# Down-projection of two wide layers in three sweeps of seven block products, with weight sums made by GpSimd during attention

## The chip, the cores and the metric

The kernel runs on one core of one Trainium2 chip. The metric is the time of one execution on the device in microseconds. Five engines work side by side, each through its own list of instructions in order: PE (TensorE, matmuls), DVE (VectorE), ACT (ScalarE), POOL (GpSimd) and SP (SyncE, which here issues most of the DMAs). An instruction that waits for a semaphore holds up everything behind it on its engine.

## The reference

The model is a small encoder over 512 tokens of width 1024: an attention layer with two head groups, a squared-ReLU MLP of width 4096, a neighbourhood attention layer, a second MLP of the same size, and a final norm, all in float32. The part in question is the MLP, which stands in both layers:

```python
def sq_relu_mlp(h, w_up, w_down):
    u = jax.nn.relu(h @ w_up)
    return (u * u) @ w_down          # w_up: 1024 x 4096, w_down: 4096 x 1024

h = x
for layer in range(DEPTH):           # DEPTH = 2
    hn = rmsnorm(h, norm_mix[layer])
    h = h + (hybrid_attention(hn, ...) if layer % 2 == 0 else neighbourhood_attention(hn, ...))
    h = h + sq_relu_mlp(rmsnorm(h, norm_ffn[layer]), ffn_w_up[layer], ffn_w_down[layer])
return rmsnorm(h, final_norm)
```

## The kernel before

Tokens lie along the free dimension: `hT` holds the residual as 8 tiles of 128 features x 512 tokens. Every float32 product is done as three matmuls: each operand is split into a rounded high half and the remainder (ACT copies the high half, DVE subtracts for the low one), and high x high, high x low and low x high are added up in PSUM (`mm3`, lines 501 to 503). So each weight chunk is loaded by SP into a raw tile, split by ACT (L212) and DVE (L202), and used by PE.

**Seven products.** Where two input tiles, two output tiles and both halves of the tokens are taken as 2 x 2 blocks, seven block products of 256 columns replace eight (class `Seven`, matmuls in L388 to L390). Weights and tokens then need sums of blocks first. In the first product of an MLP (1024 to 4096), `seven_chunk` loads two 128 x 256 weight blocks and lets GpSimd make the sums (L302 to L304); the token sums are made once.

**The MLP.** The 4096 hidden features are 32 tiles. The second product (4096 to 1024) takes them in stages: `SIZES` says how many tiles each stage has. In the first wide layer 6, 8 and 8 tiles go through the plain second product with 512-column matmuls, and 10 are kept raw (not split) and go through seven products over 256 output columns at a time, four times. In the second wide layer it is 6, 8, 6 plain, 8 raw, and 4 more tiles that the last part (`last_mlp`, `down`) takes plain, with the tokens on the partitions, so that the final norm follows from them. Beside the last plain stage, `convert` lets DVE and ACT make the sums and splits of the raw tiles.

**Attention in front.** The first attention walks through 64 steps (16 heads x 4 token blocks). A step is: scores on PE, negated maximum and scaling on DVE (L1001), exponential on ACT, reciprocal on DVE, and the scaling of the 512 probabilities of each row by GpSimd (L1005); three steps later PE transposes them (L972), and PE multiplies by the values (L985). A list of other work (`fill`) is dealt out between the steps, a share per step: projections of the second head group, then the first half of the output projection. The second half (`out_proj` with k0 = 4, again lines 501 to 503) needs the last heads and comes behind the attention, and behind it the first wide layer. The second attention has 16 heads of two half steps each (`rest`); there the order of PE, ACT, DVE and GpSimd is the order in which it is written, and GpSimd scales 256 probabilities at a time (L1430) and issues some moves of keys and queries.

**What sets the order.** Outside the second attention a scheduler orders each engine's instructions. On SP it alone does, everywhere. Weight chunks are asked for up to five chunks ahead of their use and split two ahead; a load waits for its buffer (four raw buffers, or one of 30 slots of 128 x 1024). PE's program never skips an instruction that waits.

## Time and profile before

| what | value |
|---|---|
| median of 3 runs | 1183.32 us (1182.38 to 1185.65) |
| span of the profiled execution | 1184.0 us (the page gives no other time for it) |
| PE busy | 1160.5 us, 98% |
| DVE, ACT, GpSimd busy | 883.2, 640.3, 526.1 us |
| DMA | 128.01 MB moved, 108 GB/s in the mean |
| first attention's scalings on GpSimd | 77.6 to 244.3 us |
| first matmul of the first wide layer | 267.89 us |
| second attention's scalings | 641.8 to 808.1 us |
| matmuls of L501 to L503 (512 columns) | about 0.23 us apart |

The stages in time: input projection and first attention to about 268 us, first wide layer to about 604, second attention with its projections to about 831, second wide layer to the end. A row of stretches gives the busy time of each engine in it, with PE's granted clock, the share of time in which DMA was busy, and what it moved. A row of a timeline gives the start in us, how long it took, engine, line, what it writes and reads, and in brackets how long the engine stood idle before it and what released it.

### The profile page before, as it was taken

Reading aid. Unit: us, or ns where it says so; the run is one execution under the profiler, and the core shown is the slowest. Engines: PE = TensorE matmul, PEld = TensorE weight load, DVE = VectorE, ACT = ScalarE, POOL = GpSimd, SP = SyncE. Lnnn points to the kernel's source line nnn. Section 1 sums busy time; section 2 is a strip of 40 time slices with the busy share of each in tenths; the row PEclk is TensorE's granted clock in tenths of the full one; section 3 lists DMA queues with packets and bytes.
Section 4 is the critical chain, followed back from the end, with each engine's and each line's share of the span. In section 5 each row is a group of like instructions: output and inputs, shape, how many; then the busy total and the mean of one; then the engine's idle time right before and its main releaser. Section 6 shows DMA issues by size and latency. Waiting matters only on the chain.

```text
span 1184.0 us, 19784 instructions
## 1 busy us (share of the span) xinstructions
PE 1160.5 (98%) x7128; PEld 1021.2 (86%) x7128; DVE 883.2 (75%) x1514; ACT 640.3 (54%) x1081; POOL 526.1 (44%) x662
## 2 busy tenths in 40 slices
PE   9989999999999999999999999999999999999997
PEld 8667778888899899988998998988889989998895
DVE  5788998878967368786884676667996736778975
ACT  4468676664546247562553565555554624666344
POOL 3267343224562377819602232231376625774710
PEclk9999999999999999999999999999999999999998
DMA  7223225212524723225226464433352341322412
GB/s 244 71 54 92 68 78 134 62 56 77 167 86 134 263 70 90 72 90 165 67 72 178 131 184 126 116 112 109 107 165 76 115 134 55 98 64 89 143 36 71
DMA packets 110145, 128.01 MB, mean 108 GB/s; under 512 B 9075, under 2 KB 86816, under 8 KB 110048
## 3 DMA queue, kind: packets, MB, share of 16 engines
q1 hardware_dynamic: 106992, 119.30, 33.5%
q0 software_dynamic: 2304, 6.31, 2.2%
q8 instruction: 56, 0.92, 0.3%
q10 hardware_dynamic: 752, 1.15, 0.3%
q14 instruction: 41, 0.34, 0.1%
HBM read 104.32 MB, written 6.29 MB: 93 GB/s over the span
## 4 chain that ended last, share of the span: by engine, by line
PE 81%; DVE 4%; ACT 1%; issue 1%; POOL 0%; DVEq 0%; ACTq 0%
PE mm L503 8%; PE mm L501 8%; PE mm L502 8%; PE mm L390 4%; PE mm L389 4%; PE mm L388 4%; PE t L388 3%; PE t L389 3%; PE t L390 3%; PE s L502 2%; PE s L503 2%; PE s L501 2%; PE s L390 2%; PE s L388 2%; PE s L389 2%; PE s L997 2%
## 5 line engine op out<-in xcount | busy, mean ns | idle before, releaser
L309 DVE TENSOR_TENSOR wlo<-a,whi 128x896 fp32r<-128x896 f32 x132 | 161.8, 1230 | 83.7 <-ACT whi L308 82.9
L308 ACT ACTIVATE whi<-a 128x896 fp32r<-128x896 f32 x132 | 125.0, 950 | 155.0 <-PE o L502 45.8
L501 PE MATMUL mm<-a,whi 128*128 128x512 f32 x485 | 195.9, 406 | 0.9 <-DVE a L915 0.7
L503 PE MATMUL mm<-a,wlo 128*128 128x512 f32 x485 | 192.1, 397 | 2.5 <-DVE wlo L202 2.5
L502 PE MATMUL mm<-a,whi 128*128 128x512 f32 x485 | 192.5, 397 | 0.1
L202 DVE TENSOR_TENSOR wlo<-raw,whi 128x1024 fp32r<-128x1024 f32 (+4 forms) x117 | 139.3, 1193 | 66.4 <-ACT whi L212 63.9
L212 ACT ACTIVATE whi<-raw 128x1024 fp32r<-128x1024 f32 (+3 forms) x120 | 116.4, 971 | 92.2 <-PE s L502 39.8
L302 POOL TENSOR_TENSOR a<-a 128x128 f32<-128x128 f32 x132 | 85.1, 645 | 173.3 <-DMA a<-in_ffn_w_up_dram 103.9
L303 POOL TENSOR_TENSOR a<-a 128x256 f32<-128x256 f32 x132 | 120.2, 910 | 10.3
L304 POOL TENSOR_TENSOR a<-a 128x128 f32<-128x128 f32 x132 | 115.1, 872 | 10.3
L503 PEld LDWEIGHTS mm<-a,wlo 128*128 128x128 f32 x485 | 91.7, 189 | 23.7 <-DVE wlo L202 3.4
L501 PEld LDWEIGHTS mm<-a,whi 128*128 128x128 f32 x485 | 91.8, 189 | 20.4 <-PE t L972 0.9
L502 PEld LDWEIGHTS mm<-a,whi 128*128 128x128 f32 x485 | 91.9, 190 | 17.4 <-DVE a L545 0.4
L388 PE MATMUL mm<-a,whi 128*128 128x256 f32 x370 | 103.9, 281 | 0.0
L389 PE MATMUL mm<-a,whi 128*128 128x256 f32 x370 | 103.9, 281 | 0.0
L390 PE MATMUL mm<-a,wlo 128*128 128x256 f32 x370 | 103.7, 280 | 0.0
L1005 POOL TENSOR_SCALAR p<-p,ti 128x512 f32<-128x512 f32 x64 | 46.2, 724 | 92.3 <-DVE ti L1004 81.1
L1430 POOL TENSOR_SCALAR p<-p,ti 128x256 f32<-128x256 f32 x64 | 35.6, 567 | 104.8 <-DVE ti L1429 91.8
L388 PE MATMUL t<-a,whi 128*128 128x256 f32 x264 | 74.2, 281 | 0.0
L389 PE MATMUL t<-a,whi 128*128 128x256 f32 x264 | 74.1, 281 | 0.0
L390 PE MATMUL t<-a,wlo 128*128 128x256 f32 x264 | 73.9, 280 | 0.0
L390 PEld LDWEIGHTS mm<-a,wlo 128*128 128x128 f32 x370 | 69.6, 188 | 0.2 <-DVE wlo L309 0.2
(338 smaller groups left out, 3210.8 us busy)
## 6 DMA issues: line engine op xcount, KB each, us to landing
a<-in_ffn_w_up_dram SPq DMA_DIRECT2D x104, 256.0 KB
raw<-in_ffn_w_down_dram SPq DMA_DIRECT2D x46, 512.0 KB
raw<-in_od_w_qkv_dram SPq DMA_DIRECT2D x64, 128.0 KB
a<-in_ffn_w_down_dram SPq DMA_DIRECT2D x28, 256.0 KB
raw<-in_ffn_w_up_dram SPq DMA_DIRECT2D x12, 512.0 KB
raw<-in_ev_w_in_dram SPq DMA_DIRECT2D x12, 384.0 KB
a<-a SPq DMA_DIRECT2D x18, 256.0 KB
bias<-bx SPq DMA_DIRECT2D x16, 256.0 KB
```

What stands on the lines that cost most here:

```text
L202: z = lambda: (eng or DVE).tensor_tensor(to, src, f32(high), op=ALU.subtract)
L212: ACT.activation(hi[:, 0:m], raw[:, 0:m], AF.Copy)
L303: POOL.tensor_tensor(r[:, 4:6], r[:, 2:3].to_broadcast([P, 2, P]), r[:, 0:7:6], op=ALU.add)
L304: POOL.tensor_tensor(r[:, 7], r[:, 3], r[:, 5], op=ALU.subtract)
L308: ACT.activation(hi[:, 0:896], raw[:, 128:1024], AF.Copy)
L309: DVE.tensor_tensor(lo[:, 0:896], raw[:, 128:1024], f32(hi[:, 0:896]), op=ALU.subtract)
L388: PE.matmul(o, wh, x[:, 0], start=kp == 0 and n in (0, 1, 3, 5), stop=False, skip_group_check=True)
L389: PE.matmul(o, wh, x[:, 1], start=False, stop=False, skip_group_check=True)
L390: PE.matmul(o, wl, x[:, 0], start=False, stop=kp == self.np - 1, skip_group_check=True)
L501: PE.matmul(o, wh, xh, start=first, stop=False)
L502: PE.matmul(o, wh, xl, start=False, stop=False)
L503: PE.matmul(o, wl, xh, start=False, stop=last)
```

## The change

`FIRST, RAW, MORE = 6, (26, 22), (0, 4)` takes the place of `SIZES`: in both wide layers only the first 6 tiles go through the plain second product; all others but the last 4 of the second layer are kept raw, 26 and 22 tiles, that is 13 and 11 pairs. All output columns are now handled at once: the seven products of a pair are over blocks of 512 output columns and 256 tokens, done in three sweeps over all pairs (two, two and three products), whose sums stay in six PSUM banks until a sweep ends.

The sums of the weight blocks are no longer made on the way. `SumsAhead` makes them during the attention in front: per pair of weight tiles SP loads two tiles of 512 KB, GpSimd does four additions or subtractions of 512 elements per partition, and SP writes each result (256 KB) to a buffer in DRAM (`made`), from which the second and the third sweep read; the first reads the original weights, and the third also half a tile of them. In the first attention two such steps are called per attention step from step 36 on; in the second, one after each scaling of GpSimd. The sums of token blocks are made by GpSimd in place within the sweeps, and DVE and ACT split them one pair ahead; `convert` is gone, and the transposes of the residual for the final norm move from the second product into `down`.

```diff
+    FIRST, RAW, MORE = 6, (26, 22), (0, 4)
...
+    class SumsAhead:
...
+        def load(self, kp):
+            if kp < self.n:
+                self.raw[kp] = Slot(F32), Slot(F32)
+                for z, s_ in enumerate(self.raw[kp]):
+                    k = self.k0 + 2 * kp + z
+                    SP.dma_start(s_.t, self.w[k * P : (k + 1) * P, :])
+
+        def steps(self):
+            self.load(0)
+            yield
+            for kp in range(self.n):
+                self.load(kp + 1)
...
+                POOL.tensor_tensor(a22, a21, a22, op=ALU.add)
+                SP.dma_start(line(to[0, :, S:]), a22)
+                yield
+                POOL.tensor_tensor(a21, a11, a21, op=ALU.subtract)
+                SP.dma_start(line(to[1, :, 0:S]), a21)
+                yield
+                POOL.tensor_tensor(a11, a22, a11, op=ALU.subtract)
+                SP.dma_start(line(to[0, :, 0:S]), a11)
+                yield
+                POOL.tensor_tensor(a12, a12, a11, op=ALU.subtract)
+                SP.dma_start(line(to[1, :, S:]), a12)
...
         fill.run(1.5)
+        if n >= 36:
+            next(sums0, None)
+            next(sums0, None)
...
-    SIZES = (6, 8, 8, 10), (6, 8, 6, 8, 4)
...
+    def sweep_chunk(w, k0, kind, made):
...
+        if kind == 0:
+            for z in range(2):
+                SP.dma_start(line(a[:, S * z : S * z + S]), half(k0 + z, 0))
+        else:
+            SP.dma_start(a, made[kind - 1])
+        if kind == 2:
+            SP.dma_start(line(b[:, 0:S]), half(k0 + 1, 1))
+        yield
...
+        ACT.activation(hi, a, AF.Copy)
+        DVE.tensor_tensor(lo, a, f32(hi), op=ALU.subtract)
...
+    class Sweeps:
...
+            if kind == 0:
+                split_to(d[:, :, 0], d[:, :, 1], r[:, 0:4:2])
+                POOL.tensor_tensor(r[:, 0:2], r[:, 1:4:2], r[:, 0:2], op=ALU.subtract)
+                POOL.tensor_tensor(s2, r[:, 3], r[:, 0], op=ALU.subtract)
...
+                wh, wl = hi[:, c : c + P], lo[:, c : c + P]
+                PE.matmul(o, wh, x[:, 0], start=first and m % 2 == 0, stop=False, skip_group_check=True)
+                PE.matmul(o, wh, x[:, 1], start=False, stop=False, skip_group_check=True)
+                PE.matmul(o, wl, x[:, 0], start=False, stop=last, skip_group_check=True)
...
+        reserve[0] = 3
+        sweeps = []
+        R, V = stage(0, RAW[l], MORE[l], lambda: sweeps.append(Sweeps(w, FIRST, made)))[1:]
+        reserve[0] = 6
+        beside = last(FIRST + RAW[l], V) if last else lambda kind, kp: next(bias, None)
+        for kind, kp in sweeps[0].run(R):
+            beside(kind, kp)
...
             for x in w:
                 norm(*x)
+                next(sums1, None)
```

The scheduler moves instructions around the edits. In the rows below a line number is that of the program it comes from; names are tiles, `a` being a slot.

GpSimd at the end of the first attention. Before, the last softmax scalings stand together, and the first sums of the wide layer's weights follow:

```order
L1005 TENSOR_SCALAR p_2709<-p_2709,ti_2708 128x512
L1005 TENSOR_SCALAR p_2742<-p_2742,ti_2741 128x512
L1005 TENSOR_SCALAR p_2759<-p_2759,ti_2758 128x512
L1005 TENSOR_SCALAR p_2787<-p_2787,ti_2786 128x512
L1005 TENSOR_SCALAR p_2804<-p_2804,ti_2803 128x512
L302 TENSOR_TENSOR a_3414<-a_3414 128x128
```

With the change (scaling is L1050, the four sums of a pair are L806, L809, L812 and L815):

```order
L1050 TENSOR_SCALAR p_2889<-p_2889,ti_2888 128x512
L806 TENSOR_TENSOR a_2636<-a_2635,a_2636 128x2x256
L809 TENSOR_TENSOR a_2635<-a_2635 128x2x256
L812 TENSOR_TENSOR a_2635<-a_2636,a_2635 128x2x256
L815 TENSOR_TENSOR a_2636<-a_2636,a_2635 128x2x256
L1050 TENSOR_SCALAR p_2910<-p_2910,ti_2909 128x512
L1050 TENSOR_SCALAR p_2942<-p_2942,ti_2941 128x512
L806 TENSOR_TENSOR a_2708<-a_2707,a_2708 128x2x256
L1050 TENSOR_SCALAR p_2961<-p_2961,ti_2960 128x512
L809 TENSOR_TENSOR a_2707<-a_2707 128x2x256
```

The last of these scalings is the 64th; 41 of the 52 sums stand ahead of it and 11 behind it, the first of them right behind the 35th scaling, 16 ahead of the 43rd, none between the 49th and the 55th, and 28 behind the 55th.

SP around the loads for the second half of the output projection (`raw<-in_ev_w_out_dram 128x2x512`). Before, these loads stand among the moves of keys and queries:

```order
L866 DMA a_2188<-a_2126 32x1024
L863 DMA a_2222<-a_2221 64x1024
L190 DMA raw_2880<-in_ev_w_out_dram 128x2x512
L885 DMA a_2271<-a_2270 64x1024
L866 DMA a_2221<-a_2126 32x1024
L885 DMA a_2303<-a_2302 64x1024
L887 DMA a_2270<-a_620 32x1024
L190 DMA raw_2882<-in_ev_w_out_dram 128x2x512
L887 DMA a_2302<-a_620 32x1024
L190 DMA raw_2948<-in_ev_w_out_dram 128x2x512
L190 DMA raw_2950<-in_ev_w_out_dram 128x2x512
L190 DMA raw_3065<-in_ffn_w_up_dram 128x2x512
```

With the change:

```order
L816 DMA made_621<-a_2781 128x2x256
L807 DMA made_621<-a_2842 128x2x256
L810 DMA made_621<-a_2841 128x2x256
L813 DMA made_621<-a_2841 128x2x256
L816 DMA made_621<-a_2842 128x2x256
L190 DMA raw_3037<-in_ev_w_out_dram 128x2x512
L190 DMA raw_3039<-in_ev_w_out_dram 128x2x512
L190 DMA raw_3105<-in_ev_w_out_dram 128x2x512
L190 DMA raw_3107<-in_ev_w_out_dram 128x2x512
L190 DMA raw_3222<-in_ffn_w_up_dram 128x2x512
```

All four loads now stand behind the last write of the sums; that write waits for the last sum of GpSimd.

PE at the end of the first attention. Before, matmuls of the second half of the output projection (weights `whi_2884`, from `raw_2880`) stand between transposes and value products:

```order
L972 MATMUL t_2830<-cst,p_2759 128x128 x4
L502 MATMUL mm_2878<-a_2185,whi_2884 128x512
L972 MATMUL t_2848<-cst,p_2787 128x128 x4
L503 MATMUL mm_2878<-a_2185,wlo_2885 128x512
L501 MATMUL s_2879<-a_2185,whi_2884 128x512
L502 MATMUL s_2879<-a_2185,whi_2884 128x512
L503 MATMUL s_2879<-a_2185,wlo_2885 128x512
L985 MATMUL o_2837<-a_2809,a_2310 128x256
```

With the change (weights `whi_3041`, from `raw_3037`; value products are L1030):

```order
L1030 MATMUL o_2994<-a_3003,a_2373 128x256
L1030 MATMUL o_2994<-a_3004,a_2373 128x256
L1030 MATMUL o_2994<-a_3003,a_2430 128x256
L1030 MATMUL o_2994<-a_3004,a_2430 128x256
L501 MATMUL mm_3033<-a_2232,whi_3041 128x512
L502 MATMUL mm_3033<-a_2232,whi_3041 128x512
L503 MATMUL mm_3033<-a_2232,wlo_3042 128x512
L501 MATMUL mm_3034<-a_2232,whi_3041 128x512
```

The first matmul with these weights now comes behind the last value product; to the first matmul of the wide layer the work of PE is the same in both, and up to the transposes behind the 44th scaling its order is too.

More of the change, by code (lines that the diff above doesn't have):

```diff
@@ L1094, in encoder_kernel @@
     projB(0, False)
+    ahead0 = SumsAhead(ins["ffn_w_down"][0], FIRST, RAW[0] // 2)
+    sums0 = ahead0.steps()
     attend(all_heads(), step)
+    assert next(sums0, None) is None and not ahead0.raw
     fill.until("out")
@@ L1188, in ahead, with stage @@
             state["ids"] = x7.plan(w, P * state["c"])
-        def stage(n, raw=0, more=0):
+        def stage(n, raw=0, more=0, then=lambda: None):
             if not state["plain"]:
@@ L1291, in mlp, with ev @@
-        for m in range(4):
-            def evac(w_):
-                h2 = hT[:, 2 * m : 2 * m + 2, :]
-                DVE.tensor_tensor(h2, h2, w_.t.rearrange("p (z n) -> p z n", z=2), op=ALU.add)
-            for i, _ in enumerate(u7.run(ids[m], evac)):
-                beside(m, i)
-        u7.free()
-    mlp(0)
+        U = stage(FIRST)[0]
+        up = [s_.pair() for s_ in U]
+        def ev(m, b):
+            DVE.tensor_tensor(hT[:, m, :], hT[:, m, :], b, op=ALU.add)
+        gens = [product(w, 0, up, tiles(512 * c, 512), lambda j, b, c=c: ev(4 * c + j, b)) for c in range(2)]
@@ new lines, in mlp_swept @@
+        ahead()
+        for c, gen in enumerate(gens):
+            for i, _ in enumerate(gen):
+                later(c, i)
+        for s_ in U:
+            s_.free()
+        reserve[0] = 3
[5 more added lines that the diff above has]
+            beside(kind, kp)
+        for _ in bias:
+            pass
@@ L1565, in encoder_kernel @@
         attend_C(step)
+        assert next(sums1, 0) == 0 and not ahead1.raw
         give_low(len(ready))
```

199 lines of the change are left out of this document (155 added, 44 removed).

## The prediction

> **What bounds the kernel now.** I read the page first, then stretches of time, then each engine's timeline where the edits fall. Of the page:
>
> ```profile
> span 1184.0 us, 19784 instructions
> PE 1160.5 (98%) x7128; PEld 1021.2 (86%) x7128; DVE 883.2 (75%) x1514; ACT 640.3 (54%) x1081; POOL 526.1 (44%) x662
> ```
>
> PE (TensorE) works in 98% of the span, so a shorter program on PE is time saved, provided that nothing new makes PE wait. The page gives no time for its execution beside the span of 1184.0 us; the median of the three runs, 1183.32 us, lies 0.7 us below it. My sum starts at 1184.0. Stretches give the rates (columns: from:to, length, busy time and count of PE, PEld, DVE, ACT, POOL, granted clock, DMA share, GB/s):
>
> ```profile
> 390.00:420.00 30.00, 30.00 (x130) 24.23 (x130) 10.64 (x12) 5.09 (x5) 14.49 (x24) 1.00 0.69 229
> 570.00:600.00 30.00, 30.00 (x257) 30.00 (x256) 27.89 (x33) 18.43 (x26) 12.69 (x14) 1.00 0.09 27
> 1098.00:1100.00 2.00, 2.00 (x11) 1.56 (x9) 2.00 (x4) 0.64 (x1) 0.77 (x2) 1.00 0.78 241
> 1100.00:1102.00 2.00, 0.35 (x2) 0.00 (x0) 2.00 (x3) 0.78 (x2) 1.84 (x4) 1.00 0.58 195
> 1102.00:1104.00 2.00, 1.42 (x3) 1.16 (x4) 2.00 (x3) 0.69 (x1) 1.84 (x3) 0.65 0.24 38
> 1104.00:1106.00 2.00, 2.00 (x6) 1.59 (x5) 2.00 (x4) 0.00 (x0) 1.92 (x3) 0.50 0.71 253
> ```
>
> The first stretch holds only 512-column matmuls: 30/130 = 0.2308 us each. The second holds only 256-column ones: 30/257 = 0.1167 us. The last four show the one sizeable wait of the second half, in the last wide layer: PE is idle for 1.65 + 0.58 = 2.23 us while DVE is full, and then runs at clock 0.65 and 0.50, which costs 1.42 x 0.35 + 2.00 x 0.50 = 1.5 us more.
>
> **The shorter product.** 720 matmuls of 512 columns go and 1260 of 256 come: 720 x 0.2308 = 166.2 us against 1260 x 0.1167 = 147.0 us. That is 15 pairs of raw tiles more under the seven products (8 in the first wide layer, 7 in the second), 11.08 - 9.80 = 1.28 us each. All of it is PE work on the path: **-19.2 us**.
>
> **The stall at 1100.** It comes where DVE makes sums of raw tiles beside full weight splits. The edit spreads the token splits over the sweeps. DVE was the engine waited for, so I count the whole **-3.7 us** (bounds 0 and -3.7).
>
> **Feeding the sweeps.** Groups of the two splitting engines:
>
> ```profile
> L202 DVE TENSOR_TENSOR wlo<-raw,whi 128x1024 fp32r<-128x1024 f32 x88 | 113.2, 1288 | 55.7 <-ACT whi L212 53.4 <-PE o L390 2.2
> L363 DVE TENSOR_TENSOR a<-a,a 128x512 fp32r<-128x512 f32 x51 | 41.2, 846 | 0.7 <-ACT a L362 0.7
> L336 POOL TENSOR_TENSOR a<-a 128x512 f32<-128x512 f32 x8 | 14.1, 1763 | 43.1 <-DVE a L1142 43.1
> L338 POOL TENSOR_TENSOR a<-a,a 128x256 f32<-128x256 f32 x8 | 9.4, 1174 | 0.6
> 300.00:330.00 30.00, 30.00 (x132) 24.40 (x131) 26.75 (x33) 12.46 (x19) 17.95 (x22) 1.00 0.58 184
> ```
>
> A pair in the first two sweeps is 24 x 0.1167 = 2.80 us of PE. DVE needs 1.29 + 0.85 = 2.1 us for it. GpSimd needs about 1.76 + 1.17 = 2.9 us in the first sweep, slightly more than PE, but what it makes is read a sweep later, and there it has 1.2 us of work in 2.80. DMA must bring 512 KB in 2.80 us, 187 GB/s, where the last row shows 184 GB/s with PE full. The cover is thin but real: **+2 us** for starts and ends. If DMA or DVE fell behind by 5% over some 235 us of sweeps it would be +12.
>
> **GpSimd in the first attention.** 52 sums (13 pairs, four each) go between the softmax scalings, 512 elements per partition, from the 35th of 64 scalings on. GpSimd, DVE reading two SBUF operands, and SP as they stand there now:
>
> ```profile
> 163.03 0.69 POOL L1005 TENSOR_SCALAR p<-p,ti 128x512 f32<-128x512 f32 x1 [1.01 <-DVE ti L1004]
> 163.69 2.69 POOL L202 TENSOR_TENSOR wlo<-raw,whi 128x512 fp32r<-128x512 f32 x2
> 170.19 1.16 POOL L202 TENSOR_TENSOR wlo<-raw,whi 128x256 fp32r<-128x256 f32 x2
> 178.31 1.28 POOL L202 TENSOR_TENSOR wlo<-raw,whi 128x512 fp32r<-128x512 f32 x1 [3.08 <-ACT whi L222]
> 180.23 1.29 POOL L202 TENSOR_TENSOR wlo<-raw,whi 128x512 fp32r<-128x512 f32 x1
> 182.17 1.28 POOL L562 TENSOR_TENSOR sc<-sc,a 128x512 f32<-128x512 f32 x1
> 186.04 0.70 POOL L1005 TENSOR_SCALAR p<-p,ti 128x512 f32<-128x512 f32 x1 [2.59 <-DVE ti L1004]
> 223.75 0.69 POOL L1005 TENSOR_SCALAR p<-p,ti 128x512 f32<-128x512 f32 x1 [3.26 <-PE s L997]
> ```
>
> ```profile
> 191.47 0.60 PE L972 MATMUL t<-cst,p 128*128 128x128 f32 x4
> 267.89 0.40 PE L501 MATMUL mm<-a,whi 128*128 128x512 f32 x1
> 203.93 9.15 SPq L190 DMA_DIRECT2D raw<-in_ev_w_out_dram  x2
> SPq L190 <- POOL wlo L202: 38.1, 8, 9.7
> 873.69 0.37 SPq L300 DMA_DIRECT2D a<-in_ffn_w_up_dram  x1
> 876.56 1.02 POOL L302 TENSOR_TENSOR a<-a 128x128 f32<-128x128 f32 x1 [4.05 <-DMA a<-in_ffn_w_up_dram]
> L212 ACT ACTIVATE whi<-raw 128x1024 fp32r<-128x1024 f32 x88 | 92.7, 1053 | 77.2 <-PE s L502 38.5 <-PE o L502 8.0 <-PE mm L502 7.2
> ```
>
> A sum itself is not in the trace. The rows of its size and kind in this stage take 1.28 and 1.29 us, L336 in the wide layers 1.76; these are the bounds, and I take 1.30.
>
> First, GpSimd runs late. Up to the 43rd scaling the new order has, from 163.7 on: 16 sums (20.8 us), seven scalings (4.9), the low halves (2.69 + 1.16 + 1.28 + 1.29 = 6.4) and one rotary row (1.28). That ends at 197.1, and the 43rd scaling at 197.8. PE wants it for its transposes at 191.47 at the latest (PE's order is unchanged to there), so PE waits about 6.3 us. Later PE's new order puts other work in front and hides the rest.
>
> Second, and larger, is what stands behind the sums on SP. The 55th scaling ended at 224.45; PE reaches its scores after the same work as before. Behind it GpSimd has 28 sums and nine scalings: 36.4 + 6.3 us, so the last sum ends at 267.2 if nothing was late, and at 273.4 with the 6.3. In the new order of SP all four loads of the second half of the output weights stand behind the last writes of the sums; before, the last two were issued from 203.93 on, next to the attention. SP waits for GpSimd in order, as its row of waits shows. From the last sum: issue 0.4, landing about 3.6 (256 KB landed 2.9 us after 873.69; 512 KB with others behind it takes longer), split 1.05. PE gets its first weights at 278.5 and needs 32 x 3 x 0.2308 = 22.2 us until the first matmul of the wide layer. That one moves from 267.89 to 300.7: +32.8 us, and 1.5 us for the half clock after a wait like that at 1100: **+34.3 us**, in which the 6.3 is contained. Without lateness it is +28; with sums of 1.76 us the waits are 13.7 and the last sum ends at 293.7, which gives +55. The low end holds whatever the scheduler does on PE, since PE has nothing between the last values and these weights.
>
> The Trainium skill ("SBUF — State Buffer", the part on the shared port pair) says that a GpSimd operation and a DVE one with two SBUF operands exclude each other for the whole instruction. By that rule each sum could also wait for such a DVE row; with one of 0.85 us (L363) per sum the term would be near +72. The 1.28 rows of this stage do not show it, the 1.76 of L336 does.
>
> **GpSimd and DMA in the second attention.** Here GpSimd has time: 44 sums x 1.3 = 57 us in some 115 us. DMA has less:
>
> ```profile
> 0.00:30.00 30.00, 28.94 (x141) 24.66 (x142) 15.15 (x21) 15.06 (x23) 10.33 (x18) 1.00 0.71 242
> 630.00:660.00 30.00, 30.00 (x171) 26.07 (x171) 15.99 (x45) 12.26 (x29) 9.04 (x18) 1.00 0.67 177
> 660.00:690.00 30.00, 30.00 (x188) 26.67 (x187) 21.41 (x56) 17.88 (x45) 8.76 (x16) 1.00 0.52 142
> 690.00:720.00 30.00, 30.00 (x215) 28.03 (x214) 19.90 (x57) 17.78 (x43) 7.16 (x14) 1.00 0.52 147
> 720.00:750.00 30.00, 29.84 (x184) 26.36 (x184) 20.29 (x56) 17.26 (x41) 10.73 (x20) 1.00 0.64 163
> ```
>
> The four stretches are 0.59 busy: 70 us of DMA in 120. The 11 pairs bring 11 x 2.1 MB of reads and writes; at the first row's 242/0.71 = 341 GB/s that is 68 us more, 138 in 120. Bounds: nothing, if queues and the quiet end of the stage take it up; +18, if all of it lands on PE. The weights are loaded several chunks ahead and the sums stop five heads before the end, so I take **+6 us**.
>
> The Trainium skill ("DMA: Bandwidth & Descriptors", Specifications) puts the limit of one core's HBM traffic at about 358 GB/s; this stage would ask 349, and the term would be zero. The rows here reach 253 GB/s at most.
>
> **Sum.** 1184.0 - 19.2 - 3.7 + 2 + 34.3 + 6 = 1203.4 us.
>
> **Rivals.**
> Faster: GpSimd keeps up and the weights are in time. The price that decides is that of one sum. Scalings of the same size take 0.70 us; at that price nothing is late, the last sum ends at 224.45 + 19.6 + 6.3 = 250.4, the wide layer starts 9.7 us later, and the total is 1180, or 1174 if the second attention loses nothing. The balance is at about 0.83 us per sum. Against it: every two-operand row of this size takes at least 1.28.
> No change: sums at 1.28 without lateness, neither sweeps nor second attention losing anything: 1184 - 22.9 + 28 = 1189; without the half clock (1.5) and with weights landing in 2.0 instead of 3.6 us it comes to 1186.
> Second attention bound by DMA: the +18 in place of +6 and the sweeps' +8 in place of +2: 1221. For it: 138 us of transfers in 120. Against it: PE never waits there now.
> The change does not do what it says: the sweeps run at the pace of their loads. At 160 GB/s a pair of 2.80 us takes 3.28, over 24 pairs and three sweeps about 40 us: 1240. Against it: the 229 GB/s row with PE full.
>
> **Chances.** Forecast 0.60; second attention bound 0.17; sweeps starved 0.05; no change 0.09; faster 0.09. One measurement of this kernel cannot tell 0.3% (3.5 us) from nothing. Range 1185 to 1224: the low end is the no-lateness sum, the high end takes in the bound second attention and dearer sums. Faster 0.09, same 0.09, slower 0.82.
>
> **What would show it.** Right: PE idle between the last values of the first attention and the first output-projection matmul of its second half, 10 us or more, released by a weight split that waits for DMA, with SP waiting for GpSimd; that matmul's chunk arriving after the last sum, near 273; GpSimd near full from 164 on; 256-column stretches at 257 per 30 us through all sweeps; no half clock near the end. Wrong: GpSimd's sums at 0.83 us or less, or output weights issued before the sums are done (then faster); DMA above 0.9 busy and PE waiting in the second attention or in the sweeps (then slower than 1210).

## The result and the profile after

| | before | after |
|---|---|---|
| median | 1183.1 us (1182.4 to 1185.7) | 1257.8 us (1254.9 to 1264.6) |
| ratio | | 1.063, 95% interval 1.060 to 1.067 |
| span of the profiled execution | 1184.0 us | 1253.1 us |

The change costs 74.6 us by the medians; the profiled executions differ by 69.1 us, and the working below goes by these; the profiled execution of the changed kernel lies 4.7 us below its median, so pieces of spans and medians can differ by as much. Of the page of the changed kernel:

```profile
span 1253.1 us, 21481 instructions
PE 1168.5 (93%) x7668; PEld 1051.3 (84%) x7668; DVE 916.5 (73%) x1531; ACT 679.3 (54%) x1157; POOL 665.5 (53%) x722
```

PE (TensorE) is idle for 84.6 us, where it was idle for 23.5. Its busy time grew as well, by 8.0 us, although the shorter product should have taken 19.2 off: where PE has waited, its granted clock falls (0.67 in two of the stretches below). Added up over stretches of 2 us, PE's busy time times the missing share of the clock is 23 us, against 3 before. So some 20 us of the loss, an estimate from the profile, are PE working at a lower clock beside its waits. They are spread over the four places below and are contained in the pieces of the span further down. Stretches of the changed kernel show where (columns as in the prediction: length, PE, PEld, DVE, ACT, POOL, granted clock, DMA share, GB/s):

```profile
260.00:290.00 30.00, 11.18 (x52) 8.23 (x51) 9.90 (x11) 7.76 (x11) 16.48 (x15) 0.67 0.87 276
...
540.00:560.00 20.00, 14.22 (x75) 13.31 (x76) 10.89 (x11) 6.98 (x12) 15.61 (x14) 0.67 0.65 195
...
750.00:780.00 30.00, 28.57 (x200) 25.89 (x198) 15.42 (x44) 14.11 (x33) 17.55 (x22) 1.00 1.00 312
780.00:810.00 30.00, 24.90 (x128) 21.19 (x128) 17.82 (x50) 14.99 (x36) 18.14 (x23) 0.89 0.95 268
...
1110.00:1130.00 20.00, 16.32 (x117) 16.04 (x116) 18.27 (x15) 6.73 (x11) 19.76 (x16) 0.83 0.42 143
```

Four places: the end of the first attention, the first sweep of the first wide layer, the second attention, the first sweep of the second wide layer. To give each its size I cut the span at three marks that every kernel has: M1, the first normalised tokens of the first wide layer on DVE; M2 and M3, the first and the last value product of the second attention on PE. Before:

```profile
281.12 3.79 DVE L1142 SCALAR_TENSOR_TENSOR a<-hT,gT,rb 128x512 f32<-128x512 f32 x4 [1.37 <-ACT rb L1136]
L1472 PE MATMUL o<-a,a x128: 248/277/363, 660.7 to 815.6; 128*128 128x256 f32 x64, 128*128 128x192 f32 x64
```

After:

```profile
323.28 3.78 DVE L1192 SCALAR_TENSOR_TENSOR a<-hT,gT,rb 128x512 f32<-128x512 f32 x4 [1.37 <-ACT rb L1186]
L1658 PE MATMUL o<-a,a x128: 248/278/468, 714.9 to 883.8; 128*128 128x256 f32 x64, 128*128 128x192 f32 x64
```

The first row of each pair is from the timeline, the second from the view of one line ("660.7 to 815.6": start of the first and of the last). M1 to M2 also holds the projections in front of the second attention, M3 to the end also what follows its last values.

| piece of the span, us | before | after | difference | the prediction's terms |
|---|---|---|---|---|
| start to M1: first attention | 281.1 | 323.3 | +42.2 | +34.3 |
| M1 to M2: first wide layer | 379.6 | 391.6 | +12.0 | -10.2 and a share of +2 |
| M2 to M3: second attention | 154.9 | 168.9 | +14.0 | +6 |
| M3 to end: second wide layer | 368.4 | 369.3 | +0.9 | -9.0, -3.7 and a share of +2 |

The wide layers lose 22.2 and 13.6 us beside what they should win (12.0 + 10.2 and 0.9 + 12.7): **35.8 us, where I had set +2 for the sweeps**. The other two terms are 8 us too small each.

**First attention.** The timeline of the changed kernel:

```profile
277.51 1.26 POOL L815 TENSOR_TENSOR a<-a,a 128x512 f32<-128x512 f32 x1
...
278.80 0.36 SPq L816 DMA_DIRECT2D made<-a  x1
279.21 2.04 SPq L190 DMA_DIRECT2D raw<-in_ev_w_out_dram  x4
...
285.11 0.80 PE L501 MATMUL mm<-a,whi 128*128 128x512 f32 x1 [16.42 <-ACT whi L212]
```

The last sum ends at 278.8, its write goes out, the four loads of output weights follow at once, and PE has stood for 16.4 us: the chain that was forecast, 5 us later than forecast.

**First wide layer.** The bias rows of the second attention (`bias_rows`, 56 small DMAs) stood beside the second plain stage and now come with every matmul group of the sweeps. The diff shows it in one line, and the prediction has no term for it. Waits of SP and ACT between 516 and 566 us (in total, times, longest), then SP's timeline:

```profile
SPq L1283 <- POOL a L1277: 11.3, 1, 11.3
...
ACT whi L1316 <- DMA a<-in_ffn_w_down_dram: 12.1, 3, 6.0
```

```profile
540.02 0.57 SPq L1287 DMA_DIRECT2D bx<-a  x1
540.69 1.24 SPq L1308 DMA_DIRECT2D raw<-in_ffn_w_down_dram  x2
541.98 0.62 SPq L1289 DMA_DIRECT2D bx<-a  x1
```

SP first waits 11.3 us for a copy of the bias rows that GpSimd makes behind its token sums, then spends about 0.6 us on each of the small DMAs, with the loads of the sweep between them; ACT waits 12.1 us for these loads.

**Second attention.** Waits between 690 and 870 us, then rows of the timeline:

```profile
PE t L1638 <- POOL p L1616: 8.5, 5, 3.6
...
POOL p L1616 <- DMA a<-in_ffn_w_down_dram: 7.3, 1, 7.3
```

```profile
777.49 0.21 DVE L1615 RECIPROCAL ti<-ti 128x1 f32<-128x1 f32 x2
777.84 0.48 POOL L1616 TENSOR_SCALAR p<-p,ti 128x256 f32<-128x256 f32 x1 [7.34 <-DMA a<-in_ffn_w_down_dram]
...
806.10 1.33 ACT L878 ACTIVATE a<-sc 128x512 fp32r<-128x512 f32 x2 [5.39 <-DMA made<-a]
...
812.20 0.33 PE L1638 MATMUL t<-cst,p 128*128 128x128 f32 x1 [3.64 <-POOL p L1616]
```

PE waits for scalings on GpSimd. GpSimd itself once stands for 7.3 us, and the row names the load of a sum as what ended it. But the scaling behind that wait needs the reciprocal of the row above and follows its end by about 0.2 us, as other scalings do, so the load was not what held it. The longest wait of PE, 3.64 us, can be followed back: its scaling waited for a reciprocal on DVE (at 811.00), that one for an exponential on ACT (from 807.90), and ACT had stood 5.39 us before a split, which by the profile the write of a sum (`made<-a`) released. What the shorter waits lead back to stays open.

**Second wide layer.** Groups of DVE and GpSimd from 1104 to 1134 us (busy time, mean ns, idle before):

```profile
L1317 DVE TENSOR_TENSOR wlo<-a,whi 128x1024 fp32r<-128x1024 f32 x6 | 10.9, 1834 | 0.0
L1346 DVE TENSOR_TENSOR a<-a,a 128x512 fp32r<-128x512 f32 x7 | 8.4, 1228 | 0.7 <-ACT a L1345 0.7
L1346 DVE TENSOR_TENSOR a<-a,a 128x256 fp32r<-128x256 f32 x6 | 4.5, 789 | 1.5 <-ACT a L1345 1.5
L1317 DVE TENSOR_TENSOR wlo<-raw,whi 128x1024 fp32r<-128x1024 f32 x2 | 4.3, 2162 | 0.0
L875 DVE TENSOR_TENSOR a<-a,a 128x512 fp32r<-128x512 f32 x2 | 2.3, 1212 | 0.0
...
L1352 POOL TENSOR_TENSOR a<-a 128x256 f32<-128x256 f32 x8 | 10.8, 1364 | 0.2
L1356 POOL TENSOR_TENSOR a<-a,a 128x256 f32<-128x256 f32 x8 | 9.3, 1182 | 0.2
L1351 POOL TENSOR_TENSOR a<-a 128x512 f32<-128x512 f32 x5 | 8.9, 1771 | 1.8 <-DVE a L1346 1.8
```

Both engines are full. A weight split takes 1.83 us there and a token split 1.23; I had counted 1.29 and 0.85. L1356 makes the sums that only the third sweep reads, and it runs during the first: nothing keeps GpSimd from making all sums ahead.

### The profile page after: what moved, and what is told of

The parts are those of the page before. It is cut to its first block, busy times and chain, and to the rows that moved or that the text cites. A ratio compares the mean times of both kernels' runs of the same rounds, so it can differ in the third digit from the quotient of the medians.

```text
span 1253.1 us, 21481 instructions
## 1 busy us (share of the span) xinstructions
PE 1168.5 (93%) x7668; PEld 1051.3 (84%) x7668; DVE 916.5 (73%) x1531; ACT 679.3 (54%) x1157; POOL 665.5 (53%) x722
## 4 chain that ended last, share of the span: by engine, by line
PE 64%; DVE 7%; POOL 6%; DMA 6%; issue 2%; ACT 2%; SPq 1%; POOLq 0%; DVEq 0%; ACTq 0%
PE mm L503 5%; PE mm L501 5%; PE mm L502 5%; DMA a<-in_ffn_w_down_dram 3%; PE mm L388 2%; PE mm L390 2%; PE mm L389 2%; PE t L1394 2%; PE t L1392 2%; PE t L1393 2%; PE t L388 2%; PE t L390 2%; PE t L389 2%; PE mm L1394 2%; PE mm L1393 2%
## 5 line engine op out<-in xcount | busy, mean ns | idle before, releaser
L501 PE MATMUL mm<-a,whi 128*128 128x512 f32 x395 | 162.1, 412 | 17.4 <-ACT whi L212 16.4
L309 DVE TENSOR_TENSOR wlo<-a,whi 128x896 fp32r<-128x896 f32 x98 | 124.6, 1274 | 53.0 <-ACT whi L308 51.7
L503 PE MATMUL mm<-a,wlo 128*128 128x512 f32 x395 | 157.5, 400 | 1.0 <-DVE wlo L202 1.0
L502 PE MATMUL mm<-a,whi 128*128 128x512 f32 x395 | 158.2, 400 | 0.2 <-DVE a L545 0.2
L308 ACT ACTIVATE whi<-a 128x896 fp32r<-128x896 f32 x98 | 92.9, 950 | 104.4 <-PE o L502 27.5
L202 DVE TENSOR_TENSOR wlo<-raw,whi 128x1024 fp32r<-128x1024 f32 (+4 forms) x87 | 103.4, 1193 | 51.1 <-ACT whi L212 49.6
L212 ACT ACTIVATE whi<-raw 128x1024 fp32r<-128x1024 f32 (+3 forms) x90 | 84.6, 943 | 93.2 <-PE s L502 26.6
L1317 DVE TENSOR_TENSOR wlo<-a,whi 128x1024 fp32r<-128x1024 f32 x57 | 75.8, 1333 | 43.6 <-ACT whi L1316 43.3
L302 POOL TENSOR_TENSOR a<-a 128x128 f32<-128x128 f32 x98 | 63.9, 652 | 59.8 <-DMA a<-in_ffn_w_up_dram 30.3
L304 POOL TENSOR_TENSOR a<-a 128x128 f32<-128x128 f32 x98 | 87.9, 897 | 7.7
L503 PEld LDWEIGHTS mm<-a,wlo 128*128 128x128 f32 x395 | 75.4, 191 | 19.0 <-DVE wlo L202 2.6
L1316 ACT ACTIVATE whi<-a 128x1024 fp32r<-128x1024 f32 x57 | 60.0, 1054 | 56.9 <-PE t L1393 43.4
L388 PE MATMUL mm<-a,whi 128*128 128x256 f32 x280 | 78.6, 281 | 0.0
L389 PE MATMUL mm<-a,whi 128*128 128x256 f32 x280 | 78.5, 280 | 0.0
```

Source lines behind the costliest of these rows:

```text
L202: z = lambda: (eng or DVE).tensor_tensor(to, src, f32(high), op=ALU.subtract)
L308: ACT.activation(hi[:, 0:896], raw[:, 128:1024], AF.Copy)
L309: DVE.tensor_tensor(lo[:, 0:896], raw[:, 128:1024], f32(hi[:, 0:896]), op=ALU.subtract)
L388: PE.matmul(o, wh, x[:, 0], start=kp == 0 and n in (0, 1, 3, 5), stop=False, skip_group_check=True)
L389: PE.matmul(o, wh, x[:, 1], start=False, stop=False, skip_group_check=True)
L501: PE.matmul(o, wh, xh, start=first, stop=False)
```

## The experiments

The pieces of the span in all kernels below, in us, from their profiled executions:

| kernel | to M1 | M1 to M2 | M2 to M3 | M3 to end | median |
|---|---|---|---|---|---|
| after | 323.3 | 391.6 | 168.9 | 369.3 | 1257.8 |
| e_bias | 325.8 | 383.3 | 170.2 | 369.1 | 1249.8 |
| e_late | 325.5 | 392.0 | 171.2 | 369.2 | 1258.9 |
| e_att1 | 320.5 | 390.4 | 169.2 | 369.3 | 1250.3 |
| e_att2 | 325.3 | 390.3 | 157.5 | 367.1 | 1241.6 |
| e_wout | 307.4 | 396.0 | 169.6 | 367.6 | 1243.5 |
| e_short0 | 293.1 | 395.4 | 168.4 | 369.1 | 1228.5 |
| e_third | 323.6 | 380.7 | 169.5 | 366.3 | 1244.7 |
| e_nosum | 324.6 | 370.6 | 168.8 | 356.7 | 1224.7 |
| e_only2 | 280.0 | 379.6 | 157.3 | 369.5 | 1186.7 |
| e_paced | 281.0 | 380.2 | 155.6 | 366.5 | 1184.1 |
| e_early | 280.7 | 379.7 | 155.9 | 361.9 | 1179.9 |
| e_all | 309.6 | 376.3 | 157.0 | 365.6 | 1209.6 |

Two yardsticks for the differences: a piece that an edit leaves alone varies by 2 to 3 us from kernel to kernel (to M1, 323.3 to 325.8 in the six kernels with the changed kernel's first attention), and the four runs of the changed kernel lie 10 us apart (1254.9 to 1264.6), so a gain of 5 to 8 us over its median is read together with the pieces.

### Bias rows at a fifth of the pace (e_bias)

```diff
-        beside = ... else lambda kind, kp: next(bias, None)
+        turns = iter(range(9999))
+        beside = ... else lambda kind, kp: next(turns) % 5 or next(bias, None)
```

> Only the pace of the bias rows is changed: in the sweeps of the first wide layer their next step comes with every fifth matmul group instead of with every one, so their 56 small DMAs spread over most of the three sweeps instead of the first. Theory (each such DMA costs SP 0.57 to 0.62 us of issue and the loads of the first sweep stand behind them): the stalls between 516 and 560 us go, some 17 to 20 us, 1238 to 1241 us. Rival (the first sweep is short of bandwidth, or of DVE because GpSimd sums tokens beside it, whatever SP does): the stalls stay or only move, 1254 to 1259 us.

Measured: 1249.8 us (ratio 1.056, 1.054 to 1.057), 8.0 less, all of it in the first wide layer (383.3 against 391.6). Neither figure is met. The same place now looks like the second wide layer:

```profile
540.00:560.00 20.00, 14.25 (x112) 13.22 (x111) 19.46 (x17) 8.11 (x16) 19.53 (x16) 0.99 0.83 271
```

DVE and GpSimd are full, PE is not. Two causes lay on top of each other; taken away in this order, SP's is the smaller (8.3 us here, 12.7 for the other in e_nosum).

### One token sum moved to the second sweep (e_late)

```diff
             if kind == 0:
...
-                POOL.tensor_tensor(s2, r[:, 3], r[:, 0], op=ALU.subtract)
+                if kp == self.n - 1:
+                    self.second_sum(0)
             elif kind == 1:
...
+                if kp + 1 < self.n:
+                    self.second_sum(kp + 1)
```

> Only the second of the two token sums of a pair (256 columns, s2) is moved: GpSimd makes it in the second sweep, one pair ahead of its use, instead of in the first. In the first sweep GpSimd then has one sum of about 1.76 us per pair of 2.80 us of PE instead of two of together 2.9. Theory (in the first sweep the weight splits on DVE, 1.21 us alone, stretch to 1.75 and more beside GpSimd's sums, and PE waits for them): the wide layers lose 6 to 12 us less, 1246 to 1252 us, most of it in the second one, where no bias rows are in the way. Rival (DVE has too much work of its own in the first sweep): within 3 us of 1257.8.

Measured: 1258.9 us (1.065, 1.062 to 1.068), no gain. But the edit did not do what it says. GpSimd's timeline in it (L1340 is the moved sum, L1364 the third):

```profile
1110.16 1.62 POOL L1356 TENSOR_TENSOR a<-a 128x512 f32<-128x512 f32 x1 [1.83 <-DVE a L1351]
1111.86 1.60 POOL L1340 TENSOR_TENSOR a<-a 128x256 f32<-128x256 f32 x1
...
1115.12 1.18 POOL L1364 TENSOR_TENSOR a<-a,a 128x256 f32<-128x256 f32 x1
```

The scheduler put the sum back beside the first sweep, since all that it reads is there. The run decides nothing about the cause. The next run holds a sum back by a buffer that comes free later.

### The third token sum held back by its buffer (e_third)

To e_bias this adds:

```diff
-                POOL.tensor_tensor(r[:, 2], s2, r[:, 2], op=ALU.subtract)
+                POOL.tensor_tensor(r[:, 0], s2, r[:, 2], op=ALU.subtract)
...
-                split_to(d[:, :, 0], d[:, :, 1], r[:, 1:3])
+                split_to(d[:, :, 0], d[:, :, 1], r[:, 0:2])
```

> As the kernel in which the bias rows come with every fifth group (1249.8 us), and besides the third token sum of a pair is written over the block that the second sweep's split has just read, so GpSimd cannot make it ahead of the second sweep (the products of the third sweep use the blocks in their new places). Theory (in the first sweep GpSimd's sums, 3.8 us per pair as they run ahead, lengthen DVE's splits): with a third less of them beside the first sweep, both first sweeps lose some 3 us less each, 1242 to 1246 us. Rival (DVE's own 2.5 us of splits per pair of 2.80 are too much at the start of the sweeps, whatever GpSimd does): within 2 us of 1249.8.

Measured: 1244.7 us (1.051, 1.049 to 1.052), 5.1 less than e_bias; the wide layers are 2.6 and 2.8 us shorter. The time is in the theory's range; each piece alone is hardly more than such pieces vary.

### Seven eighths of the token sums left out (e_nosum)

To e_bias this adds (32 of 256 columns; the second sum in place):

```diff
-                POOL.tensor_tensor(r[:, 0:2], r[:, 1:4:2], r[:, 0:2], op=ALU.subtract)
+                POOL.tensor_tensor(r[:, 0:2, 0:32], r[:, 1:4:2, 0:32], r[:, 0:2, 0:32], op=ALU.subtract)
```

> As the kernel in which the bias rows come with every fifth group (1249.8 us), but the three token sums of each pair in the sweeps are made over 32 of their 256 columns only and the second one in place: seven eighths of GpSimd's work in the sweeps is left out. Theory (GpSimd's sums lengthen DVE's splits, 1.75 us and more instead of 1.21): the splits of both first sweeps take 1.21 us, PE is full there, and the time is 1228 to 1234 us. Rival (DVE's own work, or the loads, set the first sweep): 1245 us or more.

Measured: 1224.7 us (1.034, 1.033 to 1.036), 25.1 less than e_bias and 3 below the lower expectation; the wide layers fall by 12.7 and 12.4 us, to 9.0 and 11.7 below before. DVE's groups in the stretch from 1080 to 1110 us, which holds its first sweep:

```profile
L1317 DVE TENSOR_TENSOR wlo<-a,whi 128x1024 fp32r<-128x1024 f32 x8 | 10.1, 1259 | 1.6 <-ACT whi L1316 1.5
L1346 DVE TENSOR_TENSOR a<-a,a 128x512 fp32r<-128x512 f32 x9 | 6.5, 741 | 0.0
L1346 DVE TENSOR_TENSOR a<-a,a 128x256 fp32r<-128x256 f32 x8 | 3.1, 422 | 1.1 <-ACT a L1345 1.0
...
L875 DVE TENSOR_TENSOR a<-a,a 128x512 fp32r<-128x512 f32 x2 | 1.5, 774 | 0.0
```

1.26 and 0.74 us instead of 1.83 and 1.23, for the same operations. So GpSimd's sums lengthen DVE's splits, and that is nearly all that the second wide layer lost (12.4 of 13.6) and over half of the loss of the first (12.7 of 22.2, with 8.3 for the bias rows).

### Sums of the second attention spread over all of it (e_att2)

```diff
                 norm(*x)
-                next(sums1, None)
+                if 7 * turns1[0] % 10 < 7:
+                    next(sums1, None)
+                turns1[0] += 1
```

> Only the pace of the sums in the second attention is changed: one after seven of ten scalings, to the end of the attention, instead of one after each of the first 44. Theory (the DMA engines are 0.95 to 1.0 busy between 720 and 810 us and the kernel's own loads come late): their share falls to about 0.9, and 8 to 13 of the 15 us lost in that stage come back, 1245 to 1250 us. Rival (the sums themselves, queued on GpSimd ahead of the next scaling, make PE wait): the waits spread as the sums do, within 4 us of 1257.8.

Measured: 1241.6 us (1.049, 1.048 to 1.051), 16.2 less; the second attention is 11.4 us shorter and keeps 2.6 of its 14.0. The 11.4 lie in the theory's 8 to 13, the time below its range. The reason is not quite the theory's:

```profile
750.00:780.00 30.00, 30.00 (x211) 27.85 (x210) 20.95 (x57) 17.33 (x42) 18.95 (x23) 1.00 0.96 290
780.00:810.00 30.00, 29.86 (x202) 27.18 (x201) 21.77 (x56) 17.62 (x41) 19.63 (x27) 1.00 0.89 234
```

DMA is still 0.96 busy in a stretch where PE is full. What is gone are the rows in which PE waits for scalings. ACT still stands once for 5.4 us until the write of a sum has landed (at 814.21), and the one longer wait that PE has left there, 1.6 us at 816.17, stands behind it. So the pace of the sums made the loss. Whether it did so by the share of DMA, by the time that their loads and writes had to land, or by the sums that stood in front of scalings, this run cannot tell.

### Earlier sums in the first attention (e_att1)

```diff
-        if n >= 36:
-            next(sums0, None)
-            next(sums0, None)
+        if n >= 22:
+            next(sums0, None)
+            if n % 3 == 0:
+                next(sums0, None)
```

> Only the start and the pace of the sums in the first attention are changed: from step 22 on, four per three steps, instead of two per step from step 36 on. Theory (GpSimd's queue is too long behind step 36, and the loads of the second half of the output weights stand on SP behind the last write): the last sum ends 15 to 26 us sooner than 278, the first matmul of the wide layer comes as much sooner than 310.3, and the time is 1232 to 1243 us. Rival (the term is set by the DMA traffic of the sums, 27 MB, or by the lock between GpSimd and DVE, which stay the same in sum): less than 8 us are won.

Measured: 1250.3 us (1.056, 1.054 to 1.058), 7.5 less, on the rival's side; M1 comes 2.8 us sooner. The timeline at the end of the attention:

```profile
275.95 0.66 PE L1017 MATMUL t<-cst,p 128*128 128x128 f32 x4 [2.74 <-POOL p L1050]
...
277.56 2.03 SPq L190 DMA_DIRECT2D raw<-in_ev_w_out_dram  x4
```

The output weights are asked for 1.6 us sooner, no more: the scalings themselves are late to the end, and M1 gains hardly more than it varies. Nor does the edit move the end: counted by its calls, the last sum is made in attention step 61 instead of 62. So an earlier start at a lighter pace wins little; what sums that end early would do, the run does not show.

### Output weights past SP (e_wout)

The second half of the output weights is loaded through ACT's queue:

```diff
-                SP.dma_start(dst, src)
+                queue.dma_start(dst, src)
...
     flip[0] = 1
+    via[0] = ACT
     for c in range(2):
         out_proj(w_out, 4, ok, [4 * c + j for j in range(4)], None)
```

> The four loads of the second half of the first attention's output weights are issued by ACT instead of SP; the sums stay as they are. Theory (these loads stand on SP behind the last write of the sums, so PE waits 16.4 us for the first of their splits): the weights are there when the last value product ends at about 268, the output projection ends at 291 instead of 310, and the time is 1239 to 1243 us against 1257.8. Rival (GpSimd's lateness in the attention itself sets the stage, or the wide layer's first weights, which stay behind the sums on SP, are waited for next): less than 6 us are won, over 1251 us.

Measured: 1243.5 us (1.049, 1.048 to 1.051), 14.3 less, at the theory's edge. M1 comes 15.9 us sooner and the 16.4 us wait is gone; 4.4 us are lost again between M1 and M2. PE now waits for the weights of the wide layer, which still stand behind the sums on SP, a part of what the rival named (timeline of SP and PE):

```profile
283.40 2.03 SPq L193 DMA_DIRECT2D raw<-in_ffn_w_up_dram  x4
...
290.83 0.50 PE L504 MATMUL mm<-a,whi 128*128 128x512 f32 x1 [3.13 <-ACT whi L215]
```

### Short sums in the first attention (e_short0)

To e_wout this adds 32 of 256 columns in the four weight sums of each pair, first attention only:

```diff
+                c = slice(0, 32 if self.k0 == 6 and self.n == 13 else 256)
-                POOL.tensor_tensor(a22, a21, a22, op=ALU.add)
+                POOL.tensor_tensor(a22[:, :, c], a21[:, :, c], a22[:, :, c], op=ALU.add)
```

> As the kernel whose output weights are loaded by ACT (1243.5 us), but the weight sums of the first attention are made over 32 of 256 columns: seven eighths of GpSimd's work for them is left out, while all their loads and writes stay. Theory (what is left of the loss in the first attention is GpSimd's time: scalings late behind sums of 1.28 to 1.9 us, and the wide layer's first weights behind the last sum): 1214 to 1222 us. Rival (the 27 MB of loads and writes, and SP waiting in order for their buffers with the moves of keys and queries behind, set the stage): 1235 us or more.

Measured: 1228.5 us (1.036, 1.034 to 1.038), 14.9 less than e_wout and between the two. M1 falls from 307.4 to 293.1, still 12.0 behind before. Rows of what remains:

```profile
200.00:220.00 20.00, 17.16 (x94) 14.16 (x93) 12.87 (x25) 10.33 (x21) 2.44 (x6) 1.00 0.84 248
220.00:240.00 20.00, 20.00 (x109) 16.36 (x108) 15.98 (x41) 12.63 (x29) 11.41 (x22) 1.00 0.99 330
...
275.86 0.79 PE L504 MATMUL mm<-a,whi 128*128 128x512 f32 x1 [3.12 <-ACT whi L215]
276.00:280.00 4.00, 3.64 (x8) 2.34 (x8) 4.00 (x6) 1.70 (x2) 1.63 (x2) 0.50 0.00 0
```

In the first stretch PE waits although GpSimd is nearly idle; in the second DMA is 0.99 busy and PE full, so a full DMA alone does not make PE wait here. The wait for the wide layer's first weights, 3.12 us, is still there. Behind it PE runs at clock 0.50 until 288 us, which costs some 5 us more (half of its busy time, an estimate). Their loads are issued at 264.35, and ACT, busy without a break from 265.68, comes to their split at 274.76: here ACT's order holds them. So of 42.2 us about 16 belong to the output weights behind the sums on SP and 14 to GpSimd's time; of the last 12 some 8, by estimate, lie at the wide layer's first weights, and how the rest divides between the traffic of the sums and SP's order no run shows.

### Only the second wide layer (e_only2)

The first wide layer and attention are as before the change; the second has the sweeps, with e_att2's pace:

```diff
-    mlp_swept(0, ahead0)
+    mlp(0)
```

> The first wide layer is as before the change (no sums in the first attention, four stages, bias rows beside the second plain stage); only the second has the three sweeps, and its sums are spread over the whole second attention, as in the kernel of 1241.6 us. Theory (the losses of the stages add up: 42.4 us in the first attention and 10.3 in the first wide layer belong to the first layer's change): 1241.6 - 52.7 = 1189, between 1185 and 1193 us, so within 0.8% of before. Rival (the second half loses less once the first half no longer runs late, or more): under 1182 us or over 1196.

Measured: 1186.7 us (1.0028, 1.0018 to 1.0038). It lies in the theory's range around 1189: the losses of the stages add up.

### Token sums held back by their buffers, second layer only (e_paced)

To e_only2 this adds a place for each sum that its own sweep has just read:

```diff
+            e = self.R[kp - 2].t.rearrange("p (b n) -> p b n", n=256)
+            return r, e[:, 0], e[:, 1]
...
+            POOL.tensor_tensor(s2, r[:, 3], r[:, 0], op=ALU.subtract)
...
+            POOL.tensor_tensor(to, s2, r[:, 2], op=ALU.subtract)
```

> As the kernel in which only the second wide layer has the sweeps (1186.7 us), but each token sum is written over a block that its own sweep has just read: the second sum of a pair can be made only in the second sweep, the third only in the third, where DVE needs 2.9 of 4.2 us per pair. Theory (each us of GpSimd's sums takes some 0.3 us from DVE, and DVE has 0.3 us to spare per pair in the first two sweeps, 1.3 in the third): 8 to 10 of the 12 to 13 us lost in that layer come back, 1176 to 1180 us, faster than before. Rival (a sum that is made just ahead of its use is late, and its split waits for GpSimd): 1183 to 1190 us.

Measured: 1184.1 us (0.9997, 0.9986 to 1.0008): no difference to before, 2.7 less than e_only2 where 8 to 10 were expected. The wait stays at the start of the first sweep:

```profile
1040.00:1050.00 10.00, 5.84 (x41) 5.44 (x40) 10.00 (x8) 2.44 (x3) 8.32 (x6) 0.90 0.58 206
```

DVE is full and PE waits. The first sum, 512 columns, is still made there, beside splits that DVE has to do for the start of the sweep. My 0.3 us per us of GpSimd was a mean over the sweep and told nothing of its start.

### Other sums, one of them made early (e_early)

To e_only2 this adds another order of four sums of 256 columns:

```diff
+            for kp in range(self.n):
+                r = self.parts(kp)
+                POOL.tensor_tensor(r[:, 1], r[:, 3], r[:, 1], op=ALU.subtract)
...
-                POOL.tensor_tensor(r[:, 0:2], r[:, 1:4:2], r[:, 0:2], op=ALU.subtract)
-                POOL.tensor_tensor(s2, r[:, 3], r[:, 0], op=ALU.subtract)
+                POOL.tensor_tensor(r[:, 0], r[:, 1], r[:, 0], op=ALU.add)
```

> As the kernel with paced token sums and sweeps in the second wide layer only (1184.1 us), but the sums are taken in another order (256 columns each): r1 = r3 - r1, which needs no block of the first sweep, is made within the first product, s2 = r1 + r0 in the first sweep, r0 = r3 - s2 in the second, s2 - r2 in the third. GpSimd then has 0.73 us per pair beside the first sweep instead of 1.28 and more. Theory (DVE is full at the start of the first sweep and GpSimd's sums lengthen its splits there): most of the 10 us still lost in that layer come back, 1175 to 1180 us, faster than before. Rival (DVE is full there because the evacuations of the first product and the splits of many pairs fall together, whatever GpSimd does): 1182 us or more.

Measured: 1179.9 us (0.9956, 0.9944 to 0.9969), **0.4% faster than the kernel before**, in the theory's range at its slow end; the kernel before took 1185.5 us beside it. The second wide layer takes 361.9 us, 6.5 less than before, and PE is busy for 17.7 of the 20 us at the start of the first sweep, where it was for 14.4 in e_paced:

```profile
1040.00:1060.00 20.00, 17.69 (x144) 16.92 (x142) 17.25 (x18) 8.07 (x14) 13.87 (x12) 1.00 0.53 186
```

### All four edits in both layers (e_all)

The edits of e_wout, e_bias, e_att2 and e_paced together in the changed kernel.

> The change with all four edits: output weights loaded by ACT's queue, bias rows with every fifth group, sums of the second attention spread over all of it, token sums paced by the sweeps. Theory (four separate losses): 1257.8 - 14.3 - 8.0 - 16.2 - 18 (2 x 9 in the two layers) = 1201, between 1196 and 1207 us; what is left is the first attention, some 28 us. Rival (one resource, DMA or GpSimd, is short throughout, and what is taken from one stage turns up in the next): 1212 us or more.

Measured: 1209.6 us (1.021, 1.018 to 1.023), between the two figures: 48.2 of 56.5 us came. Of the missing 8, more than half is e_paced's shortfall in the second wide layer (365.6 is 3.7 below 369.3, where 9 were expected). The first attention keeps 28.5 us over before.

## Why the prediction was wrong

**The sign was right, the range was not**: 1203 forecast, 1224 the upper end, 1257.8 measured. Of the signs that I had named, PE's wait for the output weights came, but the stretches of the sweeps were not full, the clock fell near the end, and DMA was above 0.9 busy with PE waiting in the second attention. Step by step:

- **The shorter product, -19.2.** Right. With the sums nearly gone and the bias rows spread (e_nosum) the wide layers are 9.0 and 11.7 us shorter than before, where -10.2 and -12.7 (with the stall) were summed.
- **The stall at 1100, -3.7.** Its cause was read right (DVE full), its end was not: a larger stall of the same kind came at the start of the sweeps.
- **Feeding the sweeps, +2.** This is the step that failed: the wide layers lost 35.8, of which the runs take back 33.4. I added up DVE's durations from rows taken elsewhere, 2.1 us per pair, and held each engine's time against PE's alone. Beside GpSimd's sums the two kinds of splits took 1.83 and 1.23 us, 3.1 per pair against PE's 2.80 (e_nosum: 25.1 us for these sums). I also wrote that the sums are read a sweep later and drew the wrong conclusion: just because nothing held them back, GpSimd made the sums of all sweeps during the first. And the bias rows, moved beside the sweeps, had no term at all (8.3 us of that stage, e_bias).
- **GpSimd in the first attention, +34.3.** The wait that I described came, the last sum 5 us later than forecast, and e_wout removes it and wins 14.3 us. But it is about 16 of the 42.2. GpSimd's lateness, which I priced at 6.3 and took as contained in the rest, makes 14 more (e_short0). Some 12 are left with the sums nearly gone, for which I had no term; in e_short0 most of them lie at the wide layer's first weights.
- **The second attention, +6.** Mis-sized: 14.0, inside its bounds. I summed DMA time over the stage; what came were late scalings, in the longest wait behind the write of a sum that held up ACT. e_att2 shows that the pace of the sums made the loss, not by which of their loads, writes and additions.
- **The clock, +1.5.** I counted it behind one wait. Over all waits the lower clock takes some 20 us more than before, an estimate that is contained in the measured pieces above.
- **The rivals.** The second attention lost 14 of the 18 us that its rival gave it, but with the sums spread DMA was nearly as full (0.96 and 0.89 after 1.00 and 0.95) and PE was full in the same stretches (e_att2), so plain saturation is not the whole of it. The sweeps did not run at the pace of their loads: e_nosum has the same loads and its wide layers are shorter than before, and right behind the stall the changed kernel's DMA moved over 400 GB/s.

```profile
564.00:568.00 4.00, 3.50 (x27) 3.30 (x28) 3.61 (x7) 2.72 (x4) 0.00 (x0) 1.00 1.02 416
568.00:572.00 4.00, 4.00 (x36) 4.00 (x36) 2.44 (x3) 2.44 (x4) 0.00 (x0) 1.00 1.03 406
```

The Trainium skill ("SBUF — State Buffer", the part on the shared port pair) has GpSimd and a two-operand DVE operation exclude each other. I weighed that rule for the attention only. It bears on the sweeps, and there the traces come near it. Among the shortest sums of the changed kernel are these:

```profile
530.87 1.29 POOL L1351 TENSOR_TENSOR a<-a 128x512 f32<-128x512 f32 x1
532.12 0.73 POOL L1356 TENSOR_TENSOR a<-a,a 128x256 f32<-128x256 f32 x1
532.81 0.73 POOL L1352 TENSOR_TENSOR a<-a 128x256 f32<-128x256 f32 x1
```

From 1104 to 1134 us DVE did 23 instructions, at e_nosum's means 8 x 1.26 + 7 x 0.74 + 6 x 0.42 + 2 x 0.77 = 19.3 us of work, and GpSimd 21, at these rows 5 x 1.29 + 16 x 0.73 = 18.1 us. Side by side that would take some 19 us, one after the other 37.4; it took 30. As an estimate, all but 0.17 us of each of the 44 instructions excluded the other engine ((37.4 - 30) / 44). By the rule a pair of the first sweep costs DVE's 1.26 + 0.74 = 2.0 us and GpSimd's 1.29 + 2 x 0.73 = 2.75 us together, 4.75 against 2.80 of PE. Over 24 pairs that is some 47 us, an upper estimate far above my bound of +12; e_nosum won 25.1.

## What to carry to other kernels

Where a change puts GpSimd work beside a DVE that is three quarters full, add the times of the two for operations that read two operands from SBUF, as the splits and sums here, instead of comparing each with PE. A step that "can be done later" is done at once by an engine with nothing else in its queue; if it must not be, write its result into a buffer that comes free later. List every DMA that moves with an edit and what stands behind it on SP, many small ones above all. Where the profile names what ended a wait, look whether another input came at the same time.

## What the runs showed of the hardware

- GpSimd's sums and DVE's splits, both with two operands in SBUF, nearly exclude each other: the weight split took 1.83 us beside the sums and 1.26 nearly without them, a sum of 256 columns 1.18 to 1.36 in the mean against 0.73. In e_nosum a sum of 32 columns (L1352) took 0.25 us at the shortest and 1.33 at the longest, about the length of a whole weight split.
- SP's issue of one DMA of the bias rows, 64 or 128 KB, took 0.57 us in the middle and up to 0.72, that of a 256 KB write of the sums (L816) 0.37 in the middle and up to 0.87.
- DMA moved 416 GB/s over 4 us at a share of 1.02, yet 312 GB/s at a share of 1.00 in the second attention: the rate alone does not tell when it is full.
- A short wait of PE costs more than its length: in e_short0 PE's clock was 0.50 from 276 to 288 us, behind waits of 3.12 and 1.20 us.
